# Bias tables of a two-block transformer kernel: one write of the table rows and 24 DRAM-to-DRAM copies in place of three broadcast writes

## The chip, the cores and the metric

One core of a Trainium2 chip. A time is the device time of one execution in microseconds; a version is given by the median of its runs, and one execution of each was also recorded by the hardware profiler. Short names: PE is the matrix engine, PEld its weight load, DVE, ACT and POOL the vector, scalar and GpSimd engines, SP the engine whose queue issues all DMAs here (SPq in the profile).

## The reference, cut to what matters

512 tokens of width 1024 go through two layers (four kinds of attention side by side, then a feed-forward of width 4096) and through a second block, whose attention has 24 heads in three groups. The second block adds to each head's logits a bias that depends on the distance between query and key alone:

```python
dist = BLOCK + i - j
bucket = t5_bucket(jnp.clip(dist, 0, n_back) * dil)
bias = jnp.transpose(bias_g[bucket].astype(jnp.float32), (2, 0, 1))   # per head, [128, 256]
logits = jnp.where(mask[None, :, None], logits + bias[None, None], -jnp.inf)
```

The feed-forward of a layer, in which the change lies, is

```python
x = x + jnp.square(jax.nn.relu(h2 @ w_up[l])) @ w_down[l]
```

## The kernel before, in words

**The weight stream.** All weights are float32 in DRAM and are used as two parts (hi and lo) whose sum they are, so each product is three matmuls (`mm3`, L159 to L161). A plan lists all weight chunks, 512 KB each for the most part, in the order of use. `send` (DMA at L123, on SP) loads a chunk into one of two `raw` buffers; `make` has ACT copy it into `whi` (L142) and POOL or, in the feed-forward, DVE subtract to get `wlo` (L143), which frees the `raw` buffer; there are four `whi` and four `wlo`. `weights` makes chunks two ahead of the one in use. Everything that is loaded or stored goes through SP's one queue.

**The feed-forward** (`ffn`, L831) runs eight blocks c = 0 to 7 per layer. A block has four chunks of `w_up`: each gives 128 of the hidden features for the 512 tokens (24 matmuls into a PSUM bank), which ACT takes out of PSUM with a relu (L849) and a square (L850), POOL squares again in full float32 (L851) and DVE turns into the low part (L852). Then four chunks of `w_down` give the products that DVE adds to x (L866). PSUM has two `acc` and two `sc` banks.

**Modulation.** In the first layer's feed-forward 24 further chunks (`w_ada`, 512 KB each) ride in the stream behind the `w_up` chunks number 4 to 27; `modulation` (L936) multiplies and sums them on DVE.

**The bias tables** (`bias_tables`, L972) are made in the first layer's feed-forward ahead of block c = 5. A [33, 24] table and a one-hot matrix (loads at L979 and L981) are multiplied (L986) into PSUM, and DVE copies the result into `tb` [24, 896] in SBUF (L987): per head one row of biases by distance, 384 numbers for the eight heads of group 0 and 256 for the sixteen of groups 1 and 2. Three DMAs (L990), one per group, write each row 128 times into the DRAM tensor `bt` [24, 128, 384]:

```python
src = tb[g * 8 : g * 8 + 8, a : a + n]
nc.sync.dma_start(self.bt[g * 8 : g * 8 + 8, :, :n], src.unsqueeze(1).to_broadcast([8, P, n]))
```

In the second block `bias_tile` (L994) reads `bt` with a row step of 383, one less than its width, so that each partition gets the row shifted by one (24 loads at L1001).

**What sets the order.** The program is written against a scheduler that orders the instructions of each engine itself by a simulated time line: the place in the source is a priority, an instruction that is ready may go ahead of earlier ones that are not, and waits and buffers are put in by it. Once ordered, an engine takes its instructions strictly in that order; on SP an instruction that waits holds all DMAs behind it, on ACT a `whi` copy that waits for its chunk holds the relu behind it.

Of the kernel before, what the change touches and what calls it, by code (L numbers as in the profile page):

```python
# [18 lines left out]
P = 128  # L19
# [38 lines left out]
class Kern:  # L58
# [25 lines left out]
    def load_x(self):  # L84
        """x and what the first products need, in the order of need; the first norm's row"""
        for b in range(NB):
            self.nc.sync.dma_start(self.x[:, b], self.t["x"][0, b * P : (b + 1) * P, :])
            if b == 0:
                g = self.row(self.t["norm1"][0])
                for _ in range(RAWS):  # L90
                    self.send()
        return g
# [21 lines left out]
    def chunk(self, ap):  # L114
        """[rows, cols] in DRAM -> [128, rows/128, cols]"""
        return ap.rearrange("(k p) c -> p k c", p=P)
# [30 lines left out]
    def weights(self, count=1):  # L147
        """the next `count` chunks of the plan, with the one behind them on its way"""
        while self.made < min(len(self.plan), self.used + count + AHEAD):
            self.make()  # L150
        got = [self.prepped.pop(self.used + i) for i in range(count)]
        self.used += count
        return got

# [1 line left out]
    def mm3(self, out, lhsT, rhs, first, last):  # L156
        """float32 product from float32r parts: lhsT and rhs are (hi, lo)"""
        mm = self.nc.tensor.matmul
        mm(out, lhsT[0], rhs[0], start=first, stop=False)  # L159
        mm(out, lhsT[0], rhs[1], start=False, stop=False)  # L160
        mm(out, lhsT[1], rhs[0], start=False, stop=last)  # L161

    def split(self, hi, lo, src, scale=None):
        """hi + lo = src (* scale), src in PSUM or SBUF"""
        if scale is None:
            self.nc.scalar.activation(hi, src, AF.Copy)  # L166
            self.nc.vector.tensor_tensor(lo, src, f(hi), ALU.subtract)  # L167
        else:
            self.nc.scalar.activation(hi, src, AF.Copy, scale=scale)
            self.nc.vector.scalar_tensor_tensor(lo, src, scale, f(hi), ALU.mult, ALU.subtract)  # L170

    def token_proj(self, hT, chunks, blk, cols):
        """[128 tokens of blk, cols]; chunks of 2 k-tiles each, stacked on the k axis"""
        out = self.psum("acc")[:, :cols]
        kts = [(c, k) for c in chunks for k in range(c[0].shape[1])]
        for n, (c, k) in enumerate(kts):
            tok = slice(blk * P, (blk + 1) * P)
            self.mm3(
                out,
                (hT[0][:, n, tok], hT[1][:, n, tok]),  # L180
                (c[0][:, k], c[1][:, k]),
                n == 0,
                n == len(kts) - 1,
            )
        return out

    def feature_proj(self, hT, chunk, at, tag="acc"):
        """[128 columns at `at` of the chunk, 512 tokens]"""
        out = self.psum(tag)
        kt = chunk[0].shape[1]  # L190
        for k in range(kt):
            self.mm3(
                out,
                (chunk[0][:, k, at : at + P], chunk[1][:, k, at : at + P]),
                (hT[0][:, k], hT[1][:, k]),
                k == 0,
                k == kt - 1,
            )
        return out

# [1 line left out]
    def rstd(self, ss, width):  # L202
        """1/sqrt(ss/width + eps)"""
# [4 lines left out]
    def rsqrt(self, v):  # L208
        """one Newton step behind exp(-ln(v)/2)"""
# [11 lines left out]
    def squares(self, dump, src, ms):  # L221
        """ms = the sum of src^2 / D"""
        self.nc.scalar.activation(dump, src, AF.Square, scale=D ** -0.5, accum_out=ms)

    def row(self, ap):
        """a DRAM row on all partitions"""
# [10 lines left out]
    def norm_to_hT(self, g):  # L237
        """normalised tokens times g, transposed"""
# [20 lines left out]
    def turn(self, hT, h, b):  # L259
        """tokens of block b, [128, 1024], into hT"""  # L260
# [27 lines left out]
    def new_v(self):  # L288
        """a head pair's values, [128 keys, block, head, hi | lo, 64]"""
        return self.att.tile([P, NB, 2, 2, 64], F32R, tag="v", name=self.name("v"), bufs=self.vbufs)  # L290

    def put_v(self, v, b, src):
        """src [128 keys, 2, 64] of a head pair"""
        self.split(v[:, b, :, 0], v[:, b, :, 1], src)

    def pv(self, out, v, x, j, th, first, last):
        """key block j's part for head x of a pair: v's high part in rows 0..63 of out, its low
        part's in rows 64..127; v of the pair; th (hi, lo) [128 keys, queries]"""
# [9 lines left out]
    def softmax(self, hd):  # L308
        """hd: q, k (hi, lo) [K, 512]; spans [(k0, n, mask)] per block; scale; sink;
        gets p, at: the normalised weights of the spans and where each starts"""  # L310
# [42 lines left out]
    def mixed_pair(self, heads, v, order):  # L353
        """two heads' attention; order: key blocks in groups that share a bank"""
# [34 lines left out]
    def total(self, pv, rows):  # L389
        """rows 0..63 plus rows 64..127 of pv, in rows of the result"""  # L390
# [8 lines left out]
    def w_out(self, mixes, tags=("acc",)):  # L399
        """x += mixed columns of two pairs @ their rows of w_out"""  # L400
# [87 lines left out]
    def indexer(self, l, hT):  # L488
        """roped queries and keys of the index; the keys transposed"""
# [35 lines left out]
    def index_scores(self, b):  # L525
        """scores of all keys for each query of block b"""
# [24 lines left out]
    def lagged(self, first, then):  # L551
        """first(b), then(b, its result) one block behind"""
# [6 lines left out]
    def topk(self, b):  # L559
        """each query's scores -> 0 where among its TOPK highest, else NEG"""  # L560
# [11 lines left out]
    def roped(self, hT, ch, sg, at, take=None):  # L572
        """256 columns of heads, 64 each, roped and transposed into pairs at, at + 1 of sg;
        with take, only 2 heads, each for both places of its pair; take(b, the rest)"""
# [51 lines left out]
    def latent_inputs(self, l, hT):  # L626
        """normalised latents, transposed; roped shared key; the up projections' weights"""
# [77 lines left out]
    def two_pairs(self, sg, vs, order, **kw):  # L705
        """attention of two head pairs: q in sg 0, 1, k in sg 2, 3"""
# [30 lines left out]
    def gated_values(self, l, hT):  # L737
        """values, and the forget gates' logarithms summed over the tokens so far"""
# [27 lines left out]
        # the negated sums, a row per block and head, by way of DRAM to all partitions  # L766
# [8 lines left out]
    def gated_keys(self, l, hT):  # L775
        """queries and keys, transposed"""
# [41 lines left out]
    def first_tiles(self, hT, chunks):  # L818
        """feature_proj of up to four chunks, the first half of the tokens before the second"""
# [11 lines left out]
    def ffn(self, l):  # L831
        nc = self.nc
        hT = self.norm_to_hT(self.row(self.t["norm2"][l]))
        for c in range(8):
# [3 lines left out]
            for n in range(4):  # L838
# [15 lines left out]
                if l == 0 and 4 * c + n in range(4, 28):  # L854
                    self.modulation(*divmod(4 * c + n - 4, KD))
# [24 lines left out]
    def first(self):  # L880
        """both layers; what the second block starts from, transposed"""
# [20 lines left out]
    def ffn_row(self, ap):  # L902
        """a DRAM row on all partitions, loaded ahead of its use"""
# [4 lines left out]
    def between(self):  # L908
        """the first block's final norm, without its factor per token: x becomes x * g,
        self.v1 the token's mean square + eps; the second block's norm and modulation, transposed"""  # L910
# [4 lines left out]
        for b in range(NB):  # L915
# [9 lines left out]
            # rstd(mean((x * g)^2) / v1) / sqrt(v1)  # L925
# [10 lines left out]
    def modulation(self, part, k):  # L936
        """what rows 128 k.. of w_ada add to `part`, from the weight stream"""
# [34 lines left out]
    def bias_tables(self):  # L972
# [3 lines left out]
        with self.tc.tile_pool(name="bias", bufs=1) as bp:  # L976
# [11 lines left out]
            for g, (a, n) in enumerate(((0, 384), (384, 256), (640, 256))):  # L988
                src = tb[g * 8 : g * 8 + 8, a : a + n]
                nc.sync.dma_start(  # L990
                    self.bt[g * 8 : g * 8 + 8, :, :n], src.unsqueeze(1).to_broadcast([8, P, n])
                )

    def bias_tile(self, h):  # L994
        """[128, 256 | 128 | 128]: what is added to head h's logits in each group"""
# [43 lines left out]
    def sigmoid(self, dst, src):  # L1039
        """1 / (1 + exp(-src))"""  # L1040
# [11 lines left out]
    def silu(self, src):  # L1052
        """src * sigmoid(src), src in PSUM"""
# [9 lines left out]
    def pair_inputs(self, hp, hT):  # L1063
        """silu(z); per group q and k, transposed, and v"""
# [13 lines left out]
        for g, which in HEADS2:  # L1078
# [3 lines left out]
            if g and which == 1:  # L1082
                # zeros beside each head's keys, so that one product takes both heads
# [23 lines left out]
    def pair_attention(self, hp, sz, qk, vs):  # L1107
# [7 lines left out]
        # where each group's and head's maxima and sums go  # L1115
# [20 lines left out]
        for i in range(NB):  # L1136
            n, scs = width(0, i), [self.psum("sc") for _ in range(2)]
            for x, y in ((0, 0), (0, 1), (1, 0)):
                # the heads' products stand on different rows of the array
# [21 lines left out]
        # the groups' maxima and sums, in the order of groups 1 and 2  # L1161
# [30 lines left out]
        # the accumulators' columns are in the order of groups 1 and 2  # L1192
# [46 lines left out]
    def pool_inputs(self, g, hT):  # L1239
        """trailing means less the tokens, silu(z); 128 channels of group g, transposed"""  # L1240
# [26 lines left out]
    def gates(self, n, hT):  # L1267
        """what the pools add to 128 merged columns, and the sigmoid on the attention's part"""
# [10 lines left out]
    def second(self, hT):  # L1279
# [4 lines left out]
        # what takes the place of x  # L1284
        aza = self.xp.tile([P, 2, 4, S], F32R, tag="x", name="aza")
        self.aza = (aza[:, 0], aza[:, 1])
        with tc.tile_pool(name="att2", bufs=1) as self.att:
# [31 lines left out]
            # what takes the place of the normalised tokens  # L1319
# [10 lines left out]
            def add(b, cs, w, k):  # L1330
                """columns cs of block b's output; k: where their mean square goes"""
# [123 lines left out]
```

## Time and profile before

| what | us |
|---|---|
| median of 3 runs | 1987.67 (1976.38 to 1988.33) |
| profiled execution, first to last instruction | 1984.9 |
| PE busy in it | 1837.7 |
| DVE, ACT, POOL busy in it | 1170.8, 850.7, 629.6 |

The page gives no other time of the profiled execution than its span, which lies 2.8 us below the median of the runs; the runs themselves spread by 12 us.

How to read the rows below: a line such as L990 is a line of the kernel, `bt<-tb` is output and input by the program's names, xN is a count. PEclk is the clock that was granted to PE, as a share of its full speed. DMA share is the mean busy share of the core's 16 DMA engines.

### The profile page before, as it was taken

What the parts mean: (1) busy time and instruction counts of PE and PEld (TensorE: products, weight loads), DVE (VectorE), ACT (ScalarE), POOL (GpSimd) and SP (SyncE); (2) the same over time, 40 slices, a digit from 0 to 9 for tenths busy, and PEclk for the clock granted to TensorE, in tenths of its full rate; (3) what the DMA queues carried; (4) which work ended last, traced back from release to release, by engine and by line L of the source; (5) the groups of instructions that cost most, each with busy time, mean ns of one, the idle gap of its engine ahead of it and who ended that gap; (6) DMA issues with size and microseconds to landing.
All of it is one profiled execution on the core that took longest, in us unless ns stands there. A gap on an engine that the chain in (4) does not pass through costs nothing.

```text
span 1984.9 us, 25692 instructions
## 1 busy us (share of the span) xinstructions
PE 1837.7 (93%) x9414; PEld 1521.6 (77%) x9414; DVE 1170.8 (59%) x2376; ACT 850.7 (43%) x1842; POOL 629.6 (32%) x425
## 2 busy tenths in 40 slices
PE   7899998999953998999998999999799999999898
PEld 6788877888842888888877888888687777877676
DVE  5899666455512536999666343433645835458674
ACT  5656764322211335656764222333434434444323
POOL 3334343111100124324432111111345544433454
PEclk9999999999976999989999999999899999999999
DMA  4222122444544413212113233333332332322242
GB/s 155 57 80 59 47 64 79 138 139 145 149 77 95 137 61 91 65 50 65 54 43 111 91 97 95 96 98 96 108 93 58 96 95 78 88 62 76 66 146 95
DMA packets 220255, 178.42 MB, mean 90 GB/s; under 512 B 14362, under 2 KB 190906, under 8 KB 220130
## 3 DMA queue, kind: packets, MB, share of 16 engines
q1 hardware_dynamic: 220130, 176.79, 30.7%
q8 instruction: 74, 1.21, 0.3%
q14 instruction: 51, 0.42, 0.1%
HBM read 168.83 MB, written 7.94 MB: 89 GB/s over the span
## 4 chain that ended last, share of the span: by engine, by line
PE 74%; DVE 13%; issue 5%; DMA 4%; ACT 2%; POOL 1%; SPq 0%; ACTq 0%; POOLq 0%; DVEq 0%
PE acc L159 18%; PE acc L161 18%; PE acc L160 18%; PE sc L159 5%; PE sc L160 4%; PE sc L161 4%; DMA raw<-in_w_down_dram 2%; PE tp L371 2%; DVE p L1202 1%; PE pv L303 1%; PE pv L302 1%; DVE b L1044 1%; DMA nrow<-neg 1%; DMA raw<-in_w_in_dram 1%; DVE bias L797 1%
## 5 line engine op out<-in xcount | busy, mean ns | idle before, releaser
L142 ACT ACTIVATE whi<-raw 128x1024 fp32r<-128x1024 f32 (+6 forms) x288 | 289.4, 1005 | 674.7 <-PE acc L160 240.1
L143 POOL TENSOR_TENSOR wlo<-raw,whi 128x1024 fp32r<-128x1024 f32 (+7 forms) x172 | 379.5, 2213 | 439.8 <-ACT whi L142 396.1
L159 PE MATMUL acc<-hTh,whi 128*128 128x512 f32 (+1 forms) x1128 | 439.2, 391 | 31.4 <-ACT tmp L849 20.3
L160 PE MATMUL acc<-hTl,whi 128*128 128x512 f32 (+1 forms) x1128 | 435.3, 386 | 2.5 <-DVE hTl L167 2.5
L161 PE MATMUL acc<-hTh,wlo 128*128 128x512 f32 (+1 forms) x1128 | 434.6, 386 | 0.0
L851 POOL TENSOR_TENSOR tmp<-tmp 128x512 f32<-128x512 f32 x64 | 101.1, 1580 | 630.7 <-ACT tmp L849 630.5
L143 DVE TENSOR_TENSOR wlo<-raw,whi 128x1024 fp32r<-128x1024 f32 x116 | 143.1, 1234 | 235.2 <-ACT whi L142 235.0
L159 PEld LDWEIGHTS acc<-hTh,whi 128*128 128x128 f32 x1128 | 215.4, 192 | 78.0 <-ACT tmp L849 21.2
L160 PEld LDWEIGHTS acc<-hTl,whi 128*128 128x128 f32 x1128 | 215.8, 191 | 42.2 <-DVE hTl L167 3.5
L161 PEld LDWEIGHTS acc<-hTh,wlo 128*128 128x128 f32 x1128 | 215.5, 191 | 40.7
L159 PE MATMUL acc<-whi,hTh 128*128 128x256 f32 (+3 forms) x512 | 156.8, 308 | 10.2 <-DVE t L280 5.3
L161 PE MATMUL acc<-whi,hTl 128*128 128x256 f32 (+3 forms) x512 | 156.2, 305 | 0.1
L160 PE MATMUL acc<-wlo,hTh 128*128 128x256 f32 (+3 forms) x512 | 154.6, 302 | 1.4 <-POOL wlo L143 1.4
L159 PE MATMUL acc<-whi,act 128*128 128x512 f32 x256 | 101.0, 400 | 33.0 <-ACT tmp L849 32.8
L159 PEld LDWEIGHTS acc<-whi,hTh 128*128 128x128 f32 x512 | 98.5, 193 | 15.8 <-issue 4.7
L160 PEld LDWEIGHTS acc<-wlo,hTh 128*128 128x128 f32 x512 | 99.0, 193 | 4.2 <-POOL wlo L143 2.1
L160 PE MATMUL acc<-wlo,act 128*128 128x512 f32 x256 | 101.9, 398 | 0.0
L161 PEld LDWEIGHTS acc<-whi,hTl 128*128 128x128 f32 x512 | 98.8, 193 | 3.8 <-issue 1.9
L159 PE MATMUL sc<-whi,act 128*128 128x512 f32 x256 | 101.6, 397 | 0.0
L160 PE MATMUL sc<-wlo,act 128*128 128x512 f32 x256 | 101.4, 396 | 0.0
L161 PE MATMUL sc<-whi,act 128*128 128x512 f32 x256 | 101.2, 396 | 0.0
L166 ACT ACTIVATE pt<-tp 128x512 fp32r<-128x512 f32 (+3 forms) x128 | 63.1, 513 | 88.3 <-PE tp L371 37.0
(333 smaller groups left out, 3590.0 us busy)
## 6 DMA issues: line engine op xcount, KB each, us to landing
raw<-in_w_in_dram SPq DMA_DIRECT2D x92, 512.0 KB, 4.1
raw<-in_w_up_dram SPq DMA_DIRECT2D x64, 512.0 KB, 4.1
raw<-in_w_down_dram SPq DMA_DIRECT2D x64, 512.0 KB, 3.3
raw<-in_w_out_dram SPq DMA_DIRECT2D x24, 512.0 KB, 3.3
raw<-in_w_ada_dram SPq DMA_DIRECT2D x24, 512.0 KB, 3.6
raw<-in_w_in_dram SPq DMA_DIRECT2D x8, 416.0 KB, 4.1
x<-in_x_dram SPq DMA_DIRECT2D x4, 512.0 KB
nrow<-neg SPq DMA_DIRECT2D x8, 256.0 KB, 3.1
```

Of the source, the lines that this page charges most:

```text
L142: self.nc.scalar.activation(hi, raw, AF.Copy)
L143: self.lo_engine.tensor_tensor(lo, raw, f(hi), ALU.subtract)
L159: mm(out, lhsT[0], rhs[0], start=first, stop=False)
L160: mm(out, lhsT[0], rhs[1], start=False, stop=False)
L161: mm(out, lhsT[1], rhs[0], start=False, stop=last)
L166: self.nc.scalar.activation(hi, src, AF.Copy)
L302: mm(out, both, th[0], start=first, stop=False)
L303: mm(out[0:64], v[:, j, x, 0], th[1], start=False, stop=False)
L371: nc.tensor.transpose(pt[:, at : at + P], hd["p"][:, src : src + P], self.ident)
L797: nc.vector.scalar_tensor_tensor(o, nrow[:, :m], cum[:, i, hh : hh + 1], self.causal[:, S - m :], ALU.add, ALU.add)
L851: nc.gpsimd.tensor_tensor(r[:, S:], r[:, :S], r[:, :S], ALU.mult)
L1044: nc.vector.reciprocal(dst, dst)
```

## The change

`bias_tables` writes `tb` once, as it is, into a new DRAM tensor `btrow` [24, 896]. A new function `bias_copy(n)` copies head n's row from `btrow` into the 128 rows of `bt[n]`, from DRAM to DRAM, with one DMA on SP. It is called 24 times in the second layer's feed-forward, behind the activations of `w_up` chunks 4 to 27 (blocks c = 1 to 6), where the first layer has its modulation. Nothing else is changed but comments.

```diff
@@ ffn
-                if l == 0 and 4 * c + n in range(4, 28):
-                    self.modulation(*divmod(4 * c + n - 4, KD))
+                if 4 * c + n in range(4, 28):
+                    if l == 0:
+                        self.modulation(*divmod(4 * c + n - 4, KD))
+                    else:
+                        self.bias_copy(4 * c + n - 4)
@@ bias_tables
-            for g, (a, n) in enumerate(((0, 384), (384, 256), (640, 256))):
-                src = tb[g * 8 : g * 8 + 8, a : a + n]
-                nc.sync.dma_start(
-                    self.bt[g * 8 : g * 8 + 8, :, :n], src.unsqueeze(1).to_broadcast([8, P, n])
-                )
+            self.btrow = self.dram.tile([24, W], F32, tag="btrow", name="btrow")
+            nc.sync.dma_start(self.btrow, tb)
+
+    def bias_copy(self, n):
+
+        g = n // 8
+        a, w = ((0, 384), (384, 256), (640, 256))[g]
+        self.nc.sync.dma_start(
+            self.bt[n, :, :w], self.btrow[n, a : a + w].partition_broadcast(P)
+        )
```

## Rows read from the trace of the kernel before

**Rows 1.** The page: the span, busy time by engine, two lines of the 40 slices.

```profile
span 1984.9 us, 25692 instructions
...
PE 1837.7 (93%) x9414; PEld 1521.6 (77%) x9414; DVE 1170.8 (59%) x2376; ACT 850.7 (43%) x1842; POOL 629.6 (32%) x425
...
PE   7899998999953998999998999999799999999898
...
PEclk9999999999976999989999999999899999999999
```

**Rows 2.** Windows of the feed-forward blocks: four of the first layer, one of the second.

```profile
core 0: us, PE busy (x) PEld busy (x) DVE busy (x) ACT busy (x) POOL busy (x), PEclk, DMA share, GB/s
...
434.20:478.80 44.60, 44.60 (x195) 36.15 (x194) 23.16 (x26) 12.97 (x16) 6.53 (x5) 1.00 0.48 142
...
568.00:630.00 62.00, 9.16 (x27) 6.61 (x25) 2.40 (x3) 3.74 (x6) 1.59 (x1) 0.58 0.44 69
630.00:674.20 44.20, 44.17 (x181) 35.65 (x182) 26.05 (x27) 15.35 (x19) 7.08 (x5) 0.94 0.52 155
...
1128.00:1172.20 44.20, 44.20 (x193) 36.06 (x192) 17.45 (x20) 12.97 (x16) 6.37 (x5) 1.00 0.32 95
```

**Rows 3.** PE's waits in 545 to 640: total us, times, longest.

```profile
PE acc L159 <- ACT tmp L849: 52.9, 2, 32.8
```

**Rows 4.** ACT's timeline from 548 to 640, the rows around the two gaps.

```profile
558.38 0.63 ACT L850 ACTIVATE act<-tmp 128x512 fp32r<-128x512 f32 x1
586.98 1.06 ACT L142 ACTIVATE whi<-raw 128x1024 fp32r<-128x1024 f32 x1 [27.97 <-DMA raw<-in_w_down_dram]
587.94 0.58 ACT L849 ACTIVATE tmp<-acc 128x512 f32<-128x512 f32 x1
...
628.43 1.06 ACT L142 ACTIVATE whi<-raw 128x1024 fp32r<-128x1024 f32 x1 [39.25 <-DMA raw<-in_w_down_dram]
629.39 0.58 ACT L849 ACTIVATE tmp<-acc 128x512 f32<-128x512 f32 x1
```

**Rows 5.** The bias writes on SP: durations least, median, most; then their sizes.

```profile
L990 SPq DMA_DIRECT2D bt<-tb x3: 798/4403/23043, 551.8 to 567.6; - x3
...
bt<-tb SPq DMA_DIRECT2D x2, 1024.0 KB
...
bt<-tb SPq DMA_DIRECT2D x1, 1536.0 KB
```

**Rows 6.** Windows of 2 us in which the bias writes alone moved.

```profile
572.00:574.00 2.00, 0.00 (x0) 0.00 (x0) 0.00 (x0) 0.00 (x0) 0.00 (x0) 0.50 0.44 50
...
600.00:602.00 2.00, 0.00 (x0) 0.00 (x0) 0.00 (x0) 0.00 (x0) 0.00 (x0) 0.89 0.42 49
```

**Rows 7.** PE's timeline behind the two gaps and behind the slow stretches.

```profile
568.14 0.39 PE L161 MATMUL acc<-hTh,wlo 128*128 128x512 f32 x1
588.57 0.80 PE L159 MATMUL acc<-hTh,whi 128*128 128x512 f32 x1 [20.04 <-ACT tmp L849]
...
594.29 0.60 PE L160 MATMUL acc<-hTl,whi 128*128 128x512 f32 x1
594.71 0.42 PE L161 MATMUL acc<-hTh,wlo 128*128 128x512 f32 x1
...
630.02 0.80 PE L159 MATMUL acc<-whi,act 128*128 128x512 f32 x1 [32.82 <-ACT tmp L849]
...
635.73 0.39 PE L160 MATMUL sc<-wlo,act 128*128 128x512 f32 x1
```

**Rows 8.** The 32 relus of each layer's feed-forward: first and last start.

```profile
L849 ACT ACTIVATE tmp<-acc x32: 576/580/599, 336.8 to 723.4; 128x512 f32<-128x512 f32 x32
...
L849 ACT ACTIVATE tmp<-acc x32: 576/579/582, 1075.3 to 1397.8; 128x512 f32<-128x512 f32 x32
```

**Rows 9.** Where loads were issued, and where what they bring is used.

```profile
L979 SPq DMA_DIRECT2D rb<-in_rel_bias_dram x1: 332/332/332, 315.2 to 315.2; - x1
...
L986 PE MATMUL acc<-oh,rb x4: 482/536/606, 549.6 to 550.8; 33*24 33x512 f32 x2, 33*24 33x384 f32 x2
...
L631 SPq DMA_DIRECT2D t<-in_mla_q_norm_dram x2: 347/388/430, 10.9 to 240.5; - x2
...
L652 DVE SCALAR_TENSOR_TENSOR tmp<-tmp,st,t x8: 338/472/2042, 772.6 to 777.7; 128x256 f32<-128x256 f32 x4, 128x128 f32<-128x128 f32 x4
```

**Rows 10.** DMAs of 128 rows: the loads of bias tiles on SP, and from issue to landing.

```profile
L1001 SPq DMA_DIRECT2D b<-bt x24: 423/432/582, 1449.4 to 1710.2; - x24
...
DMA to landing us min/median/max: 2.1/2.8/3.9
```

**Rows 11.** Windows of 1 us: broadcast loads with weights, then a store of 512 KB.

```profile
1055.00:1056.00 1.00, 0.00 (x0) 0.00 (x0) 1.00 (x1) 0.59 (x2) 1.00 (x1) 0.77 0.99 365
...
1412.00:1413.00 1.00, 1.00 (x6) 0.82 (x5) 0.90 (x2) 0.00 (x0) 1.00 (x2) 1.00 0.91 369
```

## The prediction

> **What bounds the kernel now.** I read the page first, for the busy shares: PE is busy 93% of the span, and apart from its own weight loads no engine over 59% [rows 1]. So PE's chain sets the end, and the question for any edit is where PE stands still or runs slowly. Of the page's 40 slices two neighbours stand out, the twelfth and thirteenth, where PE's digits are 5 and 3 and its granted clock 7 and 6 [rows 1], so I went to windows cut at the feed-forward blocks. A block of the first layer takes 44.6 us with PE busy in all of it; a block of the second layer takes 44.2 us, likewise full [rows 2]. Between 568 and 630 us PE worked only 9.2 of 62 us at a mean clock of 0.58 [rows 2]. That is block c = 5 of the first layer, where the bias tables are made.
>
> Who caused it is read in two steps. PE's waits of that stretch have one line that matters: 52.9 us in two waits for the relu at L849 [rows 3]. The relu was not late because of its own input: on ACT's timeline it stands right behind a `whi` copy that had waited 27.97 and then 39.25 us for a `w_down` chunk to land [rows 4]. ACT takes its instructions in order, so a late weight chunk keeps the relu from emptying the PSUM bank, and PE stops for the bank, not for the weights. The chunks were late because they were issued on SP behind the bias writes: the three DMAs at L990 held SP for 0.8, 4.4 and 23.0 us [rows 5], and while they moved alone the DMA engines carried 49 to 50 GB/s at a share of 0.42 to 0.44 [rows 6]. They bring 3.67 MB (1536 + 2 x 1024 KB, [rows 5]); at 50 GB/s that is 73 us, from 552 to about 625, which is the length of the disturbance.
>
> **The change part by part.**
>
> *Removed: the three broadcast writes.* With them go the two waits, 52.9 us [rows 3]. [...] At half clock a matmul starts every 0.42 us (594.29 to 594.71, [rows 7]), at full clock a block does 195 in 44.6 us, 0.229 us each [rows 2]. [...] Sum removed: 52.9 + 5.4 = 58.3 us. A second count confirms it: the 32 relus span 386.6 us in the first layer and 322.5 in the second [rows 8], 64.1 more; the first layer's blocks are by themselves 0.4 us longer [rows 2], some 3 us over seven blocks, and the products for the bias table, which start between 549.6 and 550.8, take another 2 [rows 9]; some 59 remain. The 58 us are all on the path, since PE is full before and behind them. They can't become more than that: a block without disturbance has no idle PE left [rows 2].
>
> *Added in the same place: one write of `tb`, 86 KB.* The nearest rows are the loads of 128 rows, 64 to 128 KB, which land 2.1 to 3.9 us after issue [rows 10]. Nothing on PE waits for it. SP waits for `tb` as before.
>
> *Added: 24 copies, and where they go.* The source puts them in the second layer, but I don't expect them there. The scheduler pulls what is ready ahead: the load of `rb`, written at block 5, was issued at 315.2 and used at 549.6; the second layer's norm row at L631 was issued at 240.5 and used first at 772.6, over 500 us and a whole feed-forward later [rows 9]. A copy needs nothing but `btrow`, and `bt` has no earlier reader. So I expect all or most of the 24 to go out on SP right behind the write of `btrow`, still in block 5 of the first layer, between its `w_down` loads. There they can delay weight chunks like the old writes, so the price depends on their pace, of which the trace has no row: nothing here goes from DRAM to DRAM.
>
> Their issue: a DMA of 128 rows holds SP for 0.432 us [rows 10], so 24 take 10.4 us. Their data: the same 3.67 MB. The bounds of the pace are 50 GB/s, the old writes into the same tensor [rows 6], and 365 GB/s, which loads that broadcast a DRAM row reached beside weight loads [rows 11]; a store to DRAM reached 369 [rows 11]. The old writes read eight rows of SBUF with less than half of the engines at work; the copies read DRAM rows, as the broadcast loads do, and write DRAM, as the store does, so I take the upper end: about 10 to 12 us for all, as long as their issue. Ahead of them SP waits for the write of `btrow`, up to 3.9 us.
>
> What a chunk may be late: ACT finished its last work at 559.0 [rows 4] and PE ran on until 568.5 [rows 7], so 9.5 us are covered by what stands ready in PSUM and in the weight buffers. If all copies stood in front of one chunk it would be 12 + 3.9 - 9.5 = 6 us too late, and if the clock fell once more up to 3 us go on top: 9. If chunks are issued between the copies, nothing: 0. I take 3, as the loads have their places in between. At the slow bound, 50 GB/s, the old 58 us come back. Below nothing the copies can't cost, since PE is full.
>
> If instead they stay in the second layer, they are 4 per block, under 1 MB beside 4 MB of weights at a DMA share of 0.32 [rows 2], and cost 0.
>
> [...]
>
> *Sum.* 1984.9 - 58.3 + 3 = 1929.6 us for the profiled execution's span; the median of the runs lies 2.8 us above it, so 1932.
>
> **The rivals.**
>
> 1. *The copies stay where they are written.* For it: their place in the source. Against it: rows 9. They cost 0: 1929.
>
> 2. *The pace per engine stays.* The old writes moved 50 GB/s at a share of 0.44, so 114 GB/s if every engine worked at that pace [rows 6]. The burst then holds all engines for 32 us, in which the weights need 0.48 of the engines' time [rows 2], 15.5 us. Chunks fall 15.5 - 9.5 = 6 us behind, 3 for the clock: 1984.9 - 58.3 + 9 + 2.8 = 1938. For it: packets of the same 1 to 1.5 KB. Against it: rows 11.
>
> 3. *The change moves the transfer and not its pace.* If what limits is the writing of short rows into `bt`, the burst takes 73 us again in the same place, and the weights wait behind it as now: 1988, no gain. For it: rows 6 are the only rows of writes into `bt`. Against it: the store of rows 11 goes to DRAM seven times as fast.
>
> 4. *Slower: a copy sits on one engine.* One engine moved 50 / (0.44 x 16) = 7.1 GB/s [rows 6]. If each copy went through a single engine at that pace, 3.67 MB would take 517 us there, and every weight chunk has a part on that engine, behind them. Pulled ahead, this is one stall of some 517 - 9.5 us: 1984.9 - 58.3 + 507 + 2.8, about 2436; within the second layer each block's four copies of 18 to 28 us would outlast its 44 us. It decides as soon as the burst takes longer than 58 + 9.5 = 68 us, below 54 GB/s. For it: the source and, for eight heads, the destination are each one contiguous piece, so that what is split could be one piece. Against it: loads of 128 rows of the same shape land in 2.8 us [rows 10].
>
> **How the numbers follow.** Forecast 0.66 (1932), rival 1 0.15 (1929), rival 2 0.10 (1938), rival 3 0.05 (1988), rival 4 0.04 (2436). A measurement of this kernel can tell about 1% from no change, 20 us. The first three are faster by more: 0.91; the third rival is within 1%: 0.05; the fourth is slower: 0.04. For the range: the low end is rival 1 less the 11 us by which one run of before lay under its median, 1918; the high end takes the worst case of the forecast (+9, 1938) and rival 2, and 14 us more for paces between 114 and 50 GB/s: 1952.
>
> **What would show each step.** Right: no wait of PE for L849 over 10 us in the first layer's feed-forward, its 32 relus in 328 to 332 us, and a full clock there; the copies issued between about 556 and 575 us, with windows at a DMA share near 1 and over 200 GB/s; `b<-bt` loads as before. Rival 1 would show the copies between 1030 and 1330 us; rival 2 windows near 114 GB/s at a share of 1; rival 3 windows of 50 GB/s and PE's two gaps again; rival 4 a share near 0.06 and one long gap. The forecast is wrong if PE's waits for L849 in block 5 still sum to more than 12 us, or if a new wait of that size stands elsewhere.

## The result, and the profile after

| | us |
|---|---|
| before, median (4 runs beside the changed kernel) | 1988.0 (1976.38 to 1989.4) |
| changed, median of 4 runs | 1935.47 (1928.96 to 1937.0) |
| changed over before | 0.9759, 95% interval 0.9734 to 0.9785 |
| span of the profiled execution, before and changed | 1984.9 and 1932.1 |

The change makes the kernel faster by 2.4%. The page of the changed kernel, span, busy time and two lines of the slices, against [rows 1]:

```profile
span 1932.1 us, 25712 instructions
...
PE 1833.3 (95%) x9414; PEld 1520.1 (79%) x9414; DVE 1172.1 (61%) x2376; ACT 850.5 (44%) x1842; POOL 627.6 (32%) x425
...
PE   7899998999999998999989999999798999999898
...
PEclk9999999999999999999999999999899999999999
```

PE does the same work in 53 us less: its idle time shrank from 147.2 to 98.8 us, its busy time by 4.4 (slow matmuls that are gone), and the two dark slices with their low clock are gone from the middle.

The relus of the two layers and PE's waits from 535 to 640, against [rows 8] and [rows 3]:

```profile
L849 ACT ACTIVATE tmp<-acc x32: 576/580/598, 339.0 to 670.5; 128x512 f32<-128x512 f32 x32
...
L849 ACT ACTIVATE tmp<-acc x32: 576/580/582, 1018.9 to 1341.4; 128x512 f32<-128x512 f32 x32
```

```profile
PE acc L159 <- DVE x L869: 2.0, 1, 2.0
PE acc L159 <- DVE tb L991: 0.7, 1, 0.7
```

The first layer's 32 relus span 331.5 us in place of 386.6; the second layer's take 322.5 us as before. The 52.9 us of waiting for the relu are gone; one new wait of 2.0 us, for an addition on DVE, stands in their place (the second line, the table's product, was there before).

SP's timeline in block 5 shows where the copies (L999) went:

```profile
557.59 0.37 SPq L123 DMA_DIRECT2D raw<-in_w_down_dram  x1
558.05 0.39 SPq L993 DMA_DIRECT2D btrow<-tb  x1
559.23 0.37 SPq L123 DMA_DIRECT2D raw<-in_w_down_dram  x1
561.76 3.77 SPq L999 DMA_DIRECT2D bt<-btrow  x6
565.58 0.59 SPq L123 DMA_DIRECT2D raw<-in_w_down_dram  x1
566.21 5.20 SPq L999 DMA_DIRECT2D bt<-btrow  x7
572.25 0.37 SPq L123 DMA_DIRECT2D raw<-in_w_down_dram  x1
572.75 6.00 SPq L999 DMA_DIRECT2D bt<-btrow  x8
578.85 0.54 SPq L123 DMA_DIRECT2D raw<-in_w_up_dram  x1
579.43 2.27 SPq L999 DMA_DIRECT2D bt<-btrow  x3
581.80 0.53 SPq L123 DMA_DIRECT2D raw<-in_w_ada_dram  x1
```

All 24 stand in the first layer, in four groups of 6, 7, 8 and 3 with a weight chunk between them. None is in the second layer, where the source has them. Windows of 2 us of that stretch, against [rows 6] (columns as in [rows 2]):

```profile
564.00:566.00 2.00, 2.00 (x11) 1.65 (x10) 0.69 (x1) 0.95 (x1) 0.61 (x1) 1.00 0.89 191
566.00:568.00 2.00, 2.00 (x10) 1.68 (x9) 1.23 (x1) 1.23 (x3) 1.32 (x1) 1.00 1.09 160
...
570.00:572.00 2.00, 2.00 (x11) 1.62 (x10) 0.00 (x0) 0.00 (x0) 0.00 (x0) 1.00 1.09 327
572.00:574.00 2.00, 2.00 (x11) 1.63 (x10) 0.61 (x1) 1.67 (x3) 0.08 (x1) 1.00 1.03 148
...
576.00:578.00 2.00, 2.00 (x10) 1.63 (x9) 0.24 (x1) 0.00 (x0) 0.00 (x0) 1.00 1.06 391
...
590.00:592.00 2.00, 2.00 (x6) 1.52 (x6) 2.00 (x3) 0.00 (x0) 0.00 (x0) 0.50 0.83 230
```

The DMA engines are full, and PE beside them is full too. In the trace, the data packets of the windows from 564, 566 and 572 all have the copies' size, 1 or 1.5 KB: the copies by themselves moved 191, 160 and 148 GB/s there, and the windows with 327 and 391 also hold packets of a weight chunk. Only at the end, behind the 2.0 us of waiting, is there a short stretch at half clock. PE's timeline there, and DVE's, which says why PE waited:

```profile
589.36 0.61 PE L159 MATMUL acc<-whi,act 128*128 128x512 f32 x1 [1.99 <-DVE x L869]
...
592.76 0.52 PE L161 MATMUL acc<-whi,act 128*128 128x512 f32 x1
```

```profile
587.42 1.28 DVE L954 SCALAR_TENSOR_TENSOR ada<-raw,cvec,ada 128x1024 f32<-128x1024 f32 x1 [5.36 <-DMA raw<-in_w_ada_dram]
588.62 0.68 DVE L869 TENSOR_TENSOR x<-acc,x 128x512 f32<-128x512 f32 x1
```

The modulation chunk issued at 581.80, the last in the line behind the copies, came late; its multiplication held DVE in order, and the addition that frees a PSUM bank stood behind it. Behind the wait, from 589.36 to 592.76, eight matmuls started 0.43 us apart in place of 0.23, which is 1.6 us more.

### The profile page after: what moved, and what is told of

Its sections match the earlier page's. It is cut to its first block, busy times and chain, and to the rows that moved or that the text cites. A ratio compares the mean times of both kernels' runs of the same rounds, so it can differ in the third digit from the quotient of the medians.

```text
span 1932.1 us, 25712 instructions
## 1 busy us (share of the span) xinstructions
PE 1833.3 (95%) x9414; PEld 1520.1 (79%) x9414; DVE 1172.1 (61%) x2376; ACT 850.5 (44%) x1842; POOL 627.6 (32%) x425
## 4 chain that ended last, share of the span: by engine, by line
PE 77%; DVE 13%; DMA 4%; ACT 2%; issue 2%; POOL 1%; SPq 0%; ACTq 0%; DVEq 0%; POOLq 0%
PE acc L159 19%; PE acc L160 19%; PE acc L161 19%; PE sc L159 5%; PE sc L160 4%; PE sc L161 4%; PE tp L371 2%; DVE p L1211 1%; PE pv L303 1%; PE pv L302 1%; DVE b L1053 1%; DMA raw<-in_w_in_dram 1%; POOL wlo L143 1%; DMA nrow<-neg 1%; DVE dsa L568 1%
## 5 line engine op out<-in xcount | busy, mean ns | idle before, releaser
L159 PEld LDWEIGHTS acc<-whi,hTh 128*128 128x128 f32 x512 | 98.6, 193 | 17.2 <-issue 4.7
```

## The experiments

My theory: the old writes cost 58 us because they held SP's queue at 50 GB/s; the copies go out in the same block and cost 3 us because they are faster. Open were what the copies cost, whether the place matters, and what had made the old writes slow: the number of engines, the tensor written, or the source in SBUF. Ratios are over the kernel before, run on the same chip.

**The floor: no copies.** The bias tiles read the table rows unshifted, so the second block gets other biases.

```diff
-                    else:
-                        self.bias_copy(4 * c + n - 4)
@@ bias_tile
-            src = bass.AP(tensor=base.tensor, offset=base.offset, ap=[[383, P], [1, n]])
+            at0 = (0, 384, 640)[g]
+            src = self.btrow[g * 8 + h, at0 : at0 + n].partition_broadcast(P)
```

> Leaves out all 24 copies; the bias tiles are read from the 24 table rows unshifted, in reads of the same shape, so the second block gets other biases. Theory (the old writes cost 58 us, the copies give back 3 to 5 us of it in block 5): about 1931, the 32 relus of the first layer in 327 to 329 us, no wait of PE in block 5 beyond the one for the table's product. Rival (the gain came from a changed order of the program elsewhere and not from the writes): no change in block 5 against the changed kernel, 1935 or more.

Measured: 1931.1 us, 0.974 (0.9705 to 0.9775). The relus:

```profile
L849 ACT ACTIVATE tmp<-acc x32: 576/580/598, 338.5 to 666.3; 128x512 f32<-128x512 f32 x32
```

They span 327.8 us. So the old writes cost 386.6 - 327.8 = 58.8 us, and the copies 331.5 - 327.8 = 3.7 (in a second profile of the changed kernel, below, 2.5). The 2.0 us of waiting and the 1.6 at half clock make up 3.6 of that 3.7. Theory held.

**The same change in the second layer.** One line: the table is made there, so nothing can be pulled ahead of it.

```diff
-            if l == 0 and c == 5:
+            if l == 1 and c == 1:
                 self.bias_tables()
```

> The table, its rows and the 24 copies are made in the second layer's feed-forward from block 1 on, since the product that they need is only asked for there; nothing is left out. Theory (a burst costs what it delays, and the second layer has no modulation chunks and a DMA share of 0.32 in place of 0.48): the copies go out in one burst there too and cost 0 to 2 us; first layer's relus in 327 to 329 us, in all about 1932. Rival (the burst costs its own length wherever it stands): 4 us again, 1935.

Measured: 1926.13 us, 0.9717 (0.9691 to 0.9743). The copies went out in one burst again, from 1048.3 to 1068.8 us. Relus of the first and the second layer:

```profile
L849 ACT ACTIVATE tmp<-acc x32: 577/580/600, 338.4 to 663.7; 128x512 f32<-128x512 f32 x32
...
L849 ACT ACTIVATE tmp<-acc x32: 576/580/590, 1007.0 to 1332.1; 128x512 f32<-128x512 f32 x32
```

The first layer's 325.3 us have neither table nor copies: the table's product by itself is 327.8 - 325.3 = 2.5 us. The second layer's 325.1 are 2.6 above the 322.5 of [rows 8], which is that product; the burst costs nothing there, as PE's waits of that stretch confirm (0.7 us, for the table). Theory held for the burst. The total is lower than it said: 1926.13 is 5.9 us under its 1932 and 5.0 under the run without copies; see below.

**From DRAM, but three DMAs with eight heads outermost.**

```diff
+            for g, (a, n) in enumerate(((0, 384), (384, 256), (640, 256))):
+                src = self.btrow[g * 8 : g * 8 + 8, a : a + n]
+                nc.sync.dma_start(
+                    self.bt[g * 8 : g * 8 + 8, :, :n], src.unsqueeze(1).to_broadcast([8, P, n])
+                )
```

> The rows are written once, and three DMAs, one per group, copy them from DRAM to DRAM with eight heads outermost, as the old writes had; nothing is left out. If the source in SBUF set the old pace, these move at 100 GB/s or more with about half of the engines, 37 us or less, and the time lies between 1935 and 1955. If the number of engines or the writing of short rows into the tensor set it, they move at 50 GB/s again, PE waits for 50 us in block 5, and the time is 1980 to 1990.

Measured: 1939.83 us, 0.9784 (0.9754 to 0.9815). A window in which they moved alone:

```profile
572.00:574.00 2.00, 2.00 (x10) 1.63 (x9) 0.00 (x0) 0.00 (x0) 0.00 (x0) 1.00 0.54 193
```

Half of the engines, as before, but 193 GB/s in place of 50: the number of engines did not set the old pace, nor did writing short rows into `bt`. PE still waits 7.2 us for a relu, because the chunks stand behind all three; the relus span 338.0 us, 6.5 more than with 24 pieces between the chunks:

```profile
L849 ACT ACTIVATE tmp<-acc x32: 576/580/598, 335.4 to 673.4; 128x512 f32<-128x512 f32 x32
```

Its four executions took 1931.81 to 1940.0 us, and the trace is of the one of 1931.81.

**From SBUF, but 24 DMAs with 128 rows outermost.**

```diff
+            for h in range(24):
+                a, w = ((0, 384), (384, 256), (640, 256))[h // 8]
+                nc.sync.dma_start(
+                    self.bt[h : h + 1, :, :w], tb[h : h + 1, a : a + w].unsqueeze(1).to_broadcast([1, P, w])
+                )
```

> 24 DMAs, one per head, each with 128 rows outermost in DRAM as in the changed kernel, but with the row in SBUF as source; nothing is left out. If the number of engines set the old pace (7 GB/s each), the pace is 114 GB/s and the time 1938 to 1945. If the row in SBUF sets it, one partition at a time gives no more than the old 50 GB/s of eight, the burst lasts 73 us or longer, and the time is 1985 or more.

Measured: 2037.72 us, 1.0276 (1.0248 to 1.0304), slower than before. One window of the burst, and PE's wait:

```profile
560.00:562.00 2.00, 2.00 (x11) 1.65 (x10) 0.00 (x0) 0.00 (x0) 0.00 (x0) 1.00 0.78 25
```

```profile
PE acc L159 <- ACT whi L142: 101.4, 1, 101.4
```

Most of the engines count as busy and move 25 to 32 GB/s for most of the burst, each DMA from one row of one partition. A high DMA share says here that packets are under way, not that much is moved. SP issued 23 of the 24 from 551.8 to 661.5 us with no chunk in between, so the chunk that PE waited for stood behind all of them.

The pace has a pattern. In windows of 4 us it rises five times in the burst, from 580, 604, 620, 636 and 652, to 44 to 51 GB/s, and falls back:

```profile
616.00:620.00 4.00, 0.00 (x0) 0.00 (x0) 0.00 (x0) 0.00 (x0) 0.00 (x0) 0.50 0.82 27
620.00:624.00 4.00, 0.00 (x0) 0.00 (x0) 0.00 (x0) 0.00 (x0) 0.00 (x0) 0.50 0.73 45
624.00:628.00 4.00, 0.00 (x0) 0.00 (x0) 0.00 (x0) 0.00 (x0) 0.00 (x0) 0.50 0.80 27
```

The distances of the rises, 24 us once and then 16 three times, are in the ratio of four long rows (384 numbers) to four short ones (256), and 24 rows have five borders between groups of four. That fits two neighbouring DMAs that overlap without gain inside a group of four partitions and with gain across a border.

**The old three writes with the rows spread.** What one row gives is 27 GB/s for the most part and what eight neighbours give is 50, so neighbours seemed to share something. The rows of a group are put four partitions apart by the order of the columns in the product, with 32 columns in place of 24; the DMAs are those of before, with SBUF as the source.

```diff
-                src = tb[g * 8 : g * 8 + 8, a : a + n]
+                src = tb[g : g + 29 : 4, a : a + n]
```

> The three old writes from SBUF, in the first layer's block 5, with one thing changed: the eight rows of a group stand on partitions four apart (0 to 28) in place of eight neighbours, so that each row has a group of four partitions to itself; the product for the table has 32 columns in place of 24; nothing is left out. Theory A (what limits a read from SBUF is shared by four neighbouring partitions: one row gave 27 GB/s, eight neighbours, two such groups, 50): the writes move at 150 GB/s or more, PE waits less than 15 us in block 5, in all 1930 to 1945. Theory B (each repeated row is slow by itself, 6 to 7 GB/s): 50 GB/s again, PE waits 50 us, 1978 to 1988.

Measured: 1933.06 us, 0.9761 (0.9727 to 0.9796). That is the gain of the change (0.9759), as far as the interval tells, without its DRAM-to-DRAM copies. A window of the writes, PE's wait and the first layer's relus:

```profile
564.00:566.00 2.00, 2.00 (x11) 1.65 (x10) 0.61 (x1) 1.67 (x3) 0.08 (x1) 1.00 0.54 194
```

```profile
PE acc L159 <- ACT tmp L849: 4.7, 1, 4.7
```

```profile
L849 ACT ACTIVATE tmp<-acc x32: 575/580/597, 336.2 to 671.5; 128x512 f32<-128x512 f32 x32
```

The relus span 335.3 us, 3.8 to 5.0 more than with the copies: the writes go out in three large pieces, and PE's wait is 4.7 us in place of 2.0. Theory A held: 194 GB/s with the same shape and the same share of engines (0.54) as the run from DRAM. The paces agree with a limit that belongs to a group of four neighbouring partitions: one row gave 27 GB/s, so an estimate for two groups is 54 and for eight 216, and 50 and 194 were measured; the five rises of the per-head run agree too. What the four partitions share, no run shows. Other distances between the rows, 2 or 8 or 32 partitions, were not tried.

**The old writes in the second layer.** The first two experiments' place with the old writes.

> The three old writes from SBUF, unchanged, but table and writes in the second layer's feed-forward at block 1; nothing is left out. Theory (their pace of 50 GB/s holds SP's queue for 73 us wherever they stand, and a chunk can be 10 us late): PE stands still for 45 to 60 us in that block of the second layer, the first layer's relus take 325 us, in all 1970 to 1990. Rival (the modulation chunks of the first layer made the old writes costly, and the second layer's free DMA share takes them): a stall under 20 us, 1925 to 1950.

Measured: 1980.17 us, 1.0002 (0.9987 to 1.0018), no gain. PE's waits in the second layer's feed-forward:

```profile
PE acc L159 <- ACT tmp L849: 49.5, 3, 30.6
```

The place alone changes nothing; the pace is what counts.

**Twice the copies.** Each head's row goes into a second tensor too, which nobody reads.

```diff
+        for t in (self.bt, self.bt2):
+            self.nc.sync.dma_start(t[n, :, :w], self.btrow[n, a : a + w].partition_broadcast(P))
```

> Each head is copied twice, into two tensors, of which the second is not read: 48 copies, 7.3 MB, in the first layer's block 5 and behind; nothing is left out. Theory (a copy costs only what it makes a chunk late beyond the cover of some 10 us): the burst lasts 40 us or longer, chunks fall behind by more than with 24, and PE loses 8 to 25 us in blocks 5 and 6 in place of 4: 1938 to 1958. Rival (the copies are hidden beside the weights at any number, and the 4 us are the wait for the rows): 1935 to 1937, relus in 331 to 333 us.

Measured: 1946.2 us, 0.9834 (0.981 to 0.9858). The relus, and PE's waits in 535 to 700:

```profile
L849 ACT ACTIVATE tmp<-acc x32: 577/581/599, 335.8 to 684.6; 128x512 f32<-128x512 f32 x32
```

```profile
PE acc L159 <- DVE x L869: 11.3, 1, 11.3
PE acc L159 <- ACT tmp L849: 4.3, 3, 2.2
```

They span 348.8 us, 21 above the floor where 24 copies cost 2.5 to 3.7: the price rises far more than in proportion. That fits a cost behind a cover: the first 24 copies nearly use it up, and the next 24, a second 3.67 MB, are paid for with some 17 us (348.8 - 331.5).

**Where the rest of the second-layer version's gain lies.** Two runs on one chip: the changed kernel once more, and the second-layer version with its table product in two other PSUM banks.

> The changed kernel itself, beside the next one on the same chip, since the second-layer version came out 9 us below it where its burst saves only 3 to 4 us in block 5. Theory (the rest of the 9 us is spread between runs in the attention stages): 1930 to 1937 and the two medians 3 to 6 us apart. Rival (the second-layer version is faster in other stages too, by its order): 8 us or more apart again.

```diff
-                o = self.psum("acc")
+                o = self.psum("tp")
```

> Table and copies in the second layer, as in the second-layer version, and the product for the table into the two spare transposition banks in place of the two banks that the feed-forward turns over; nothing is left out. Theory (the product costs 2.5 us, of which PE's wait for the bank is 0.7 and the matmuls themselves 1.7): second layer's relus in 324 to 325 us in place of 325.1, in all 1924 to 1928. Rival (the product's whole 2.5 us is the banks): relus in 323 us.

Measured: the changed kernel 1931.05 us, 0.9758 (0.9735 to 0.9781); the other 1922.49 us, 0.971 (0.9688 to 0.9733), the fastest version here. They are 8.6 us apart, so the rival held that the second-layer version gains elsewhere too. Its relus and where its product stands:

```profile
L849 ACT ACTIVATE tmp<-acc x32: 577/580/590, 1007.8 to 1330.7; 128x512 f32<-128x512 f32 x32
```

```profile
L990 PE MATMUL tp<-oh,rb x4: 482/544/606, 1004.1 to 1008.4; 33*24 33x512 f32 x2, 33*24 33x384 f32 x2
```

322.9 us, not the 324 to 325 that I expected: with free banks the scheduler pulled the product ahead to 1004 us, to where the feed-forward starts up, so that it lies mostly ahead of the first relu. The guess that its matmuls had to be paid was wrong. The spans of the two profiles, 1928.9 and 1920.9, are 8.0 us apart. The larger part of it lies in the first layer's relus, 330.3 and 325.2 us:

```profile
L849 ACT ACTIVATE tmp<-acc x32: 574/581/601, 335.8 to 666.1; 128x512 f32<-128x512 f32 x32
...
L849 ACT ACTIVATE tmp<-acc x32: 577/580/599, 337.0 to 662.2; 128x512 f32<-128x512 f32 x32
```

These 5.1 us are the copies and the table's product, 2.5 each, which the second version doesn't have there and in the second layer has nearly for nothing. Another 4.1 lie in the second layer's attention (307.7 and 303.6), and the other stages take 1.2 back. The attention is measured from the last multiplication with the norm's row ahead of it to the last one behind it, here before and changed:

```profile
L251 DVE SCALAR_TENSOR_TENSOR tmp<-x,st,tmp x24: 740/744/753, 7.6 to 1065.5; 128x512 f32<-128x512 f32 x24
L251 DVE SCALAR_TENSOR_TENSOR tmp<-x,st,row x8: 739/745/754, 737.5 to 755.2; 128x512 f32<-128x512 f32 x8
```

```profile
L251 DVE SCALAR_TENSOR_TENSOR tmp<-x,st,tmp x24: 741/746/753, 7.7 to 1009.1; 128x512 f32<-128x512 f32 x24
L251 DVE SCALAR_TENSOR_TENSOR tmp<-x,st,row x8: 743/748/754, 684.7 to 702.4; 128x512 f32<-128x512 f32 x8
```

The last start of the first line less that of the second: 310.3 us before, 306.7 changed. In the eight profiles of before, the changed kernel (twice), the floor, the three DMAs from DRAM, the writes per head, the double copies and the spread rows it is 303.1 to 310.3; in the three with the table in the second layer 302.4 to 303.6. Put side by side, the programs of before and of the change have the same order of PE's matmuls except in the first layer's blocks 5 and 6, and the second-layer version has another through the second layer's attention. So the same order takes between 303 and 310 us, and the other order was never above 304. Why the first one scatters was not tried and stays open.

## Why the prediction was right, point by point

The forecast was 1932 in 1918 to 1952; the medians are 1935.47 and, in a second series, 1931.05.

- *What the old writes cost.* Forecast 58.3 us (52.9 of waiting, 5.4 of half clock); the run without copies shows 58.8. All of it came back, as forecast from the blocks' being full of PE work. The 5.4 can be read from the trace of before: from 588.57 to 594.71 and from 630.02 to 635.73, 11.85 us, the granted clock was 0.50 and PE started 14 matmuls in each stretch, and 28 at the 0.229 us of a full block would take 6.4. About half of it is the 3 us that the forecast allowed for one more fall of the clock; in the changed kernel that fall cost 1.6.
- *Where the copies go.* Forecast: in the first layer's block 5, behind the write of the rows, between the `w_down` loads, 556 to 575 us. They stand there, 561.8 to 581.7, between those loads but some 6 us later. Rival 1, the second layer, is out for the program as written; made true by force, it saves what the burst costs.
- *What they cost.* Forecast 3 of 0 to 9; measured 2.5 to 3.7. That is in part luck: the 3 was chosen between the bounds and not worked out, and the parts were less exact than the sum. An issue held SP 0.596 us (the median), not the 0.432 of [rows 10], and the four groups sum to 17.2 us of issue, not 10.4; the write of the rows held the first copy to 561.76, 3.7 us from its issue, near the 3.9 allowed; a copy landed after 5.5 us (median). From the first copy's issue to the end of the last group are 20 us, where the forecast had 10 to 12. With 20, its own worst case would have been 20 + 3.7 - 9.5 = 14 us of lateness and not 6. Chunks between the copies were what kept it at 3: the three undivided DMAs cost 10.2.
- *By which way they cost it.* The forecast saw a late chunk holding a relu on ACT. It was a modulation chunk, holding an addition on DVE (2.0 us) and then 3.4 us at half clock, where the forecast's sign was a full clock. The step was the same, the engine another, and it would explain why the second layer, which has no such chunks, pays nothing. Its lower DMA share (0.32 in [rows 2]) would explain that as well: 0.32 of a burst of 23 us is 7 us of weights, less than the 9.5 of cover. No run tells the two apart.
- *The pace.* This term was mis-sized. I took it near the 365 GB/s of [rows 11]; the windows that hold copies alone show 148 to 191 at a share of 0.89 to 1.09. The 327 and 391 of other windows count a weight chunk too. With about all engines at work the copies were not faster than the three DMAs on half of them (193), so the number of engines doesn't set their pace either; what does stays open. The windows of [rows 11] moved packets of 4 KB, the copies' have 1 to 1.5 KB; whether that matters was not tried. Of my two reasons the first holds in part: the rows in DRAM are read faster than eight neighbouring rows of SBUF (193 GB/s in place of 50), but SBUF as such is not slow (194 with the rows spread). The second, less than half of the engines at work, does not hold. Rival 2 (each engine keeps its 7 GB/s) falls with the three DMAs, in which half of the engines move 193, but its way of counting was the better one: at 160 GB/s the burst is 23 us, the weights need 0.48 of it, 11, and 11 - 9.5 leaves an estimated 1.5 us of lateness, where PE's wait was 2.0. Rival 3 (the writes into `bt` are slow) falls with the same run, rival 4 with the windows.
- *The stage times.* Against the span the forecast was 1929.6 and the profile has 1932.1. The first layer's relus are within it (331.5, forecast 328 to 332). The 2.5 us are a balance of stages outside the first layer's feed-forward: 2.2 more ahead of the first relu (339.0 against 336.8), 3.5 less between the two layers' relus (348.4 against 351.9), 3.6 more behind the last one (590.7 against 587.1). Each is as large as the 3 us of the copies, so that the sum came within 2.5 us of the span is in part luck too.

## What to carry to other kernels

A broadcast out of a few neighbouring SBUF rows was slow in both cuts tried, 50 GB/s with three DMAs and 25 to 32 for the most part with 24, where spread rows gave 194 and rows in DRAM 193: look at the GB/s of a window in which it moves alone, and spread the rows over partitions or take them from DRAM. A transfer in SP's queue was paid here only for what it made the next load late beyond its cover (an estimated 9.5 us, from [rows 4] and [rows 7]): the old writes, some 73 us long, cost 58.8 and the copies, 20 us with chunks between them, 2.5 to 3.7. So the cover should be read first, from the last work of the engine that waits to the end of PE's. A place in the source is not a place in time where a scheduler pulls ready DMAs forward; to move a transfer, move what it depends on.

## What the runs showed of the hardware that I had not expected

- The pace of a read from SBUF by the place of its rows: 25 to 32 GB/s for most of a burst that reads row by row with most engines busy, 44 to 51 where such a burst passes from one group of four rows to the next, 50 from eight neighbours, 194 from eight rows four partitions apart.
- DRAM to DRAM with each row read 128 times: 193 GB/s on half of the engines, like the spread rows of SBUF (194), and no more on about all of them (148 to 191).
- A high DMA share says little of the pace: 0.78 stood beside 25 GB/s, 1.06 beside 391.
